# Retention part of a two-layer decoder: weight blocks asked for one ahead, head ends 24 products behind the sums, later modulations

## The chip, the cores and the metric

The kernel runs on 1 core of one Trainium2 chip. The metric is the device time of one execution in microseconds. Before the change the median of 3 runs is 2658.96 us (2655.59 to 2659.36).

## The reference

Two layers on a sequence of 256 rows of width 2048. Layer 0 mixes with retention (8 heads, key width 256, value width 512), layer 1 with a short gated convolution; each is followed by a SwiGLU part of width 5632. Every sub-layer is normalised, scaled and shifted by rows made from a conditioning vector `c`, and its output is multiplied by a gate made the same way.

```python
c_act = jax.nn.silu(c)
for i in range(DEPTH):
    mod = (c_act @ w_mod[i] + b_mod[i])[:, None, :]
    sh1, sc1, g1, sh2, sc2, g2 = jnp.split(mod, 6, axis=-1)
    h = (rms_norm(x, norm1_g[i]) * (1.0 + sc1) + sh1).astype(x.dtype)
    ...
    x = (x + g1 * y).astype(x.dtype)
    h = (rms_norm(x, norm2_g[i]) * (1.0 + sc2) + sh2).astype(x.dtype)
    x = (x + g2 * swiglu(h, ffn_w_in[i], ffn_w_out[i])).astype(x.dtype)

def retention_mixer(h, cos, sin, w_in, w_out):
    q, k, v, g = jnp.split(h @ w_in, [qk_w, 2 * qk_w, 2 * qk_w + v_w], axis=-1)
    q = rope(split_heads(q, RET_HEADS), cos, sin)
    k = rope(split_heads(k, RET_HEADS), cos, sin) * (RET_DK ** -0.5)
    v = split_heads(v, RET_HEADS)
    ...
    o = rms_norm(chunked_gated_linear_attention(q, k, v, log_a))
    return ((jax.nn.silu(g) * merge_heads(o)) @ w_out).astype(h.dtype)
```

## The kernel before

All activations lie with features on the 128 partitions and the 256 rows along the free axis, as 16 tiles. Two streams come from memory, both as 1 MB blocks of 128 x 2048 float32, all issued on SP's queue. `w_all` (456 blocks) holds every weight of a product in the order of use. `w_mod` (192 blocks) holds the matrix for the conditioning rows; each of these blocks is reduced to one column by a VectorE multiply-and-sum (L244, in `modulation`), followed by a small addition on GpSimd. 32 of them belong to the start; the other 160 are spread over the kernel by `paced`, which follows `plan_mod`: pairs of (units of product done, modulations due), interpolated between them. A unit is one product of a 128 x 128 weight tile; the retention part has 2048 of them. They are issued at lower priority (`MOD_PRIO`).

**The weight stream.** A product needs each weight in two parts. `prepare` takes half a block (1024 columns): ScalarE makes `hi` by a cast (L310), VectorE makes `lo = raw - hi` (L313). `take` keeps two halves (`AHEAD`) ready ahead of the one in use. `fetch` asks for a block: it takes the next of the 3 buffers of the tag `raw` (`RAW_BUFS`), whose turn goes round strictly, and issues the transfer on SP. The buffers of `w_mod` blocks have the same tag, so a block of either kind takes the buffer of the block three before it, and its transfer waits until that one's last reader is done. In the first spans (up to `early`) `prepare` asks for up to two blocks beyond the one in use; after that only when a block is needed.

**Order of work.** TensorE's order is written out by hand. VectorE's and ScalarE's orders are the scheduler's, except in the start and the first spans, where they are by hand too; every engine works through its own order in sequence. `product` runs two matmuls for each weight tile (L355 with hi, L358 with lo), `packed` three (L378, L379, L380), the values of a head three wide ones (L801, L802, L803).

**The retention part.** First some spans of columns of several heads (`RET_SPANS`, 480 units), while the rows are being normalised. Then the heads in the order 4, 0, 2, 1, 5, 3, 6, 7. `projections` does, for each head: the pair for q and its rotation (`rope`, L778 to L786 on VectorE), the pair for k, the values, the scores, two more pairs for the gate. What is left of a head, its *asides* from `mixed`, runs inside the next head's products: `outputs(0)` and `outputs(1)` (score times value, L847 and L850, and sums of squares), `roots` (sums over partitions on TensorE, L413; VectorE L422; the power on GpSimd, L424) and `ends` (L431 spreads the roots over the partitions; then for each of four tiles VectorE multiplies, L864, ScalarE casts, L394, and VectorE takes the rest, L395, into a `mid` tile named `rm`). `ticked`, called after every k step of a product with the number of products done, runs the next aside when so many have passed as its entry in `STEPS` says: 8, 8, 24, 12.

After four heads and after eight, `ret_out` multiplies by the output weights (`output`, `RET_OUT`): its first group makes 6 columns over 12 of the 16 k steps (72 products), while the last head's asides run; then a group for each of these columns adds the last 4 k steps, which read the four `rm` tiles of that last head; then the other columns follow over all 16.

Of the kernel before, what the change touches and what calls it, by code (L numbers as in the profile page):

```python
# [17 lines left out]
P = 128  # L18
D = 2048
S = 256  # L20
KT = D // P
# [24 lines left out]
MOD_LEAD = 64  # L46
MOST = 0.045
MOD_PRIO = -300
STEPS = (8, 8, 24, 12)
RAW_BUFS = 3  # L50
PART_BUFS = 4

# [80 lines left out]
def in_use_order():  # L133

    for g in RET_SPANS:
        yield "ret_w_in", 0, g
    for n, h in enumerate(HEAD_ORDER):
        qkg, v = RET_HEADS[h]
        for g in qkg[:2] + [v] + qkg[2:]:
            yield "ret_w_in", 0, g  # L140
        if n % (HEADS // 2) == HEADS // 2 - 1:
            for g in RET_OUT[n // (HEADS // 2)]:
                yield "ret_w_out", 0, g
    for layer in range(DEPTH):
        if layer == 1:
            for g in CONV_IN:
                yield "conv_w_in", 0, g
            for g in CONV_OUT:
                yield "conv_w_out", 0, g
        for part in range(2):  # L150
            for g in FFN_IN[part]:
                yield "ffn_w_in", layer, g
            for g in FFN_OUT[part]:
                yield "ffn_w_out", layer, g
# [31 lines left out]
def trunk(ctx: ExitStack, tc: tile.TileContext, x_in, c_in, pos_in, w_mod, cols_in, tab_in, w_all, out):  # L186
# [8 lines left out]
    def name(s):  # L195
        serial[0] += 1
        return f"{s}_{serial[0]}"
# [62 lines left out]
    n_mod = len(todo)  # L260
    todo.reverse()
    first = len(RET_SPANS[0].cols) * FIRST_KS
    early = sum(len(g.cols) * len(g.ks) for g in RET_SPANS)
    plan_mod = [(early, 0), (1024, 18), (1984, 49), (5184, 9 * KT), (5888, n_mod)]
    units, allowed = [0], [0.0]

    def paced(n):
# [19 lines left out]
    ready, taken_cols, raws, fetched, n_fetched = [], [0], [], [], [0]  # L287

    def fetch():
        raw = wpool.tile([P, CHUNK], F32, tag="raw", name=name("raw"), bufs=RAW_BUFS)  # L290
        nc.sync.dma_start(raw, w_all[n_fetched[0]])
        n_fetched[0] += 1
        fetched.append(raw)

    def prepare(between=None):
        n = prepared[0]
        if n == n_halves:
            return
        prepared[0] += 1
        i = n * HALF % CHUNK  # L300
        if i == 0:
            if not fetched:
                fetch()
            raws[:] = [fetched.pop(0)]
            while first <= units[0] < early and len(fetched) < RAW_BUFS - 1 and n_fetched[0] < w_all.shape[0]:
                fetch()
        raw = raws[0][:, i : i + HALF]
        hi = wpool.tile([P, HALF], F32R, tag="hi", name=name("hi"))
        lo = wpool.tile([P, HALF], F32R, tag="lo", name=name("lo"))
        nc.scalar.copy(hi, raw)  # L310
        if between:
            between()
        nc.vector.tensor_tensor(lo, raw, hi.bitcast(F32), op=ALU.subtract)  # L313
        ready.append((hi, lo))
# [3 lines left out]
    def take(group, k, col):  # L318

        assert order.pop() == (group, k, col)  # L320
        i = taken_cols[0] % HALF
        if i == 0:
            if ready and taken_cols[0]:
                ready.pop(0)
            while len(ready) < 1 + AHEAD * (units[0] >= first):
                n = len(ready)
                prepare()
                if len(ready) == n:
                    break
        taken_cols[0] += group.width  # L330
        return [t[:, i : i + group.width] for t in ready[0]]
# [211 lines left out]
    with ExitStack() as inner:  # L543
# [64 lines left out]
        with tc.tile_pool(name="start", bufs=1) as sp:  # L608
# [56 lines left out]
            with tc.manual_schedule(engines={mybir.EngineType.DVE, mybir.EngineType.Activation}):  # L665
# [59 lines left out]
                def before(k):  # L725
                    low = []
                    prepare(lambda: low.append(row(k)))
                    low[0]()

                pts = packed(RET_SPANS[0], h, before=before, between=both_reduced, banks=banks)  # L730
                prepare()
                prepare()
                for i, pt in enumerate(pts):
# [103 lines left out]
        def mixed(head, both, v, sg):  # L837
# [3 lines left out]
            def outputs(half):  # L841
                for i in range(2 * half, 2 * half + 2):
                    pt = bank()
                    w = slice(i * P, (i + 1) * P)
                    for jt, sp in enumerate(both):
                        at = slice(jt * P, S)
                        nc.tensor.matmul(  # L847
                            pt[:, :, at], v[:, jt, 0, w], sp, start=jt == 0, stop=False, skip_group_check=True
                        )
                        nc.tensor.matmul(  # L850
                            pt[:, 1, at], v[:, jt, 1, w], sp[:, 0, :], start=False, stop=jt == 1, skip_group_check=True
                        )
                    o = summed(pt, rp.tile([P, S], F32, tag="o", name=name("o"), bufs=4))
                    accs[0] = squares(accs[0], o, "hacc")
                    nc.vector.tensor_tensor(o, o, sg[i], op=ALU.mult)
                    os.append(o)
# [11 lines left out]

            return list(zip(STEPS, [lambda: outputs(0), lambda: outputs(1), roots, ends]))

# [153 lines left out]
```

## Time and profile before

| what | us |
|---|---|
| median of 3 runs | 2658.96 |
| profiled execution | 2658.37 |
| its span | 2656.6 |
| VectorE busy in the span | 2019.6 |
| ScalarE busy in the span | 1260.2 |
| L313, lo: 912 of them, mean | 1.223 |
| L310, hi: 912 of them, mean | 1.050 |
| L244, modulation: 160 of them, mean | 2.285 |
| block of `w_all`, issue to landing, median | 4.9 |
| block of `w_mod`, issue to landing, median | 5.2 |

The table is read from the page's first, fifth and sixth parts. Mean durations include the start-up of an instruction, which overlaps with its neighbour when they run back to back, so a row of three L313 in 3.49 us costs less than three times the mean. The granted clock of TensorE is 0.996 of full speed over the span. The transfers' queue took 69.4% of what 16 DMA engines could give.

In time, the first spans end at about 215 us, heads 4, 0, 2 and 1 run until 350 us, the first `ret_out` until 443 us, heads 5, 3, 6 and 7 until 709 us, and the second `ret_out` to about 800 us. A head's asides are at the start of its follower: L431 of head 4 stands at 250 us, of head 0 at 287, of head 2 at 335.7, of head 1 at 373.7 and of head 5 at 537.7.

### The profile page before, as it was taken

The page shows a single profiled execution, that of the slowest core. Times are in us where ns is not written, and L with a number is a line of the kernel's source. Part 1 is how long each engine was busy: PE and PEld are TensorE (multiplying, and loading weights), DVE is VectorE, ACT ScalarE, POOL GpSimd, SP SyncE. Part 2 cuts the span into 40 slices and gives each one's busy share as a digit, 9 for nine tenths or more (in the row PEclk, how much of TensorE's full clock was granted, in tenths as well). Part 3 has the DMA queues.
Part 4 walks back from the last instruction along what each step waited for, and adds up shares of the span by engine and source line. Part 5 has one row for each costly group of instructions (what it writes and reads, how often), then busy time and mean ns, then how long its engine had stood idle before and what let it go on. Part 6 is the DMA issues. An engine that isn't in the chain of part 4 may idle for free.

```text
span 2656.6 us, 40105 instructions
## 1 busy us (share of the span) xinstructions
PE 2619.1 (99%) x16044; PEld 2337.2 (88%) x16044; DVE 2019.6 (76%) x2646; ACT 1260.2 (47%) x1819; POOL 152.5 (6%) x230
## 2 busy tenths in 40 slices
PE   7999999999999999999999999999999999999998
PEld 6998889889889888888888898888988888888887
DVE  7888988787699877777777889878887665555554
ACT  5545543444456444344444454444554443444443
POOL 0000000120000011100000001100000000000000
PEclk9999999999999999999999999999999999999999
DMA  9975668777676877877777758777777765555553
GB/s 396 396 274 221 221 234 317 260 271 280 242 272 252 322 282 262 300 268 279 283 278 274 274 218 322 288 276 262 264 267 260 263 222 190 187 185 185 188 190 127
DMA packets 96958, 687.70 MB, mean 259 GB/s; under 512 B 10753, under 2 KB 12545, under 8 KB 13825
## 3 DMA queue, kind: packets, MB, share of 16 engines
q1 hardware_dynamic: 96770, 685.13, 69.4%
q8 instruction: 125, 2.05, 0.3%
q14 instruction: 63, 0.52, 0.1%
HBM read 682.99 MB, written 2.10 MB: 258 GB/s over the span
## 4 chain that ended last, share of the span: by engine, by line
PE 75%; issue 19%; DVE 3%; DMA 2%; ACT 0%; POOL 0%; DVEq 0%; SPq 0%; ACTq 0%; POOLq 0%
PE bank L355 35%; PE bank L358 17%; PE bank L380 4%; PE bank L378 4%; PE bank L379 4%; PE bank L802 2%; PE bank L803 2%; PE bank L801 2%; PE bank L494 1%; PE bank L493 1%; PE bank L495 1%; DMA raw<-w_all 1%; DVE lo L313 1%; DMA raw<-w_mod 0%; DVE raw L244 0%
## 5 line engine op out<-in xcount | busy, mean ns | idle before, releaser
L313 DVE TENSOR_TENSOR lo<-raw,hi 128x1024 fp32r<-128x1024 f32 x912 | 1112.1, 1223 | 548.1 <-ACT hi L310 544.1
L310 ACT CAST hi<-raw 128x1024 fp32r<-128x1024 f32 x912 | 953.9, 1050 | 1099.7 <-PE bank L355 630.8
L355 PE MATMUL bank<-h,hi 128*128 128x512 f32 x3296 | 1155.2, 395 | 0.0
L358 PE MATMUL bank<-h,lo 128*128 128x256 f32 x3296 | 924.4, 280 | 0.0
L355 PEld LDWEIGHTS bank<-h,hi 128*128 128x128 f32 x3296 | 622.6, 189 | 145.3
L358 PEld LDWEIGHTS bank<-h,lo 128*128 128x128 f32 x3296 | 622.0, 189 | 0.0
L355 PE MATMUL bank<-mid,hi 128*128 128x512 f32 x1604 | 556.3, 393 | 0.0
L358 PE MATMUL bank<-mid,lo 128*128 128x256 f32 x1604 | 444.9, 277 | 0.0
L244 DVE SCALAR_TENSOR_TENSOR raw<-raw,cb 128x2048 f32<-128x2048 f32 x160 | 365.6, 2285 | 10.8 <-DMA raw<-w_mod 10.3
L355 PEld LDWEIGHTS bank<-mid,hi 128*128 128x128 f32 x1604 | 300.7, 187 | 69.4
L358 PEld LDWEIGHTS bank<-mid,lo 128*128 128x128 f32 x1604 | 301.3, 188 | 0.1
L380 PE MATMUL bank<-h,lo 128*128 128x256 f32 x1024 | 291.1, 284 | 7.5 <-DVE lo L313 7.5
L378 PE MATMUL bank<-h,hi 128*128 128x256 f32 x1024 | 291.0, 284 | 3.6 <-ACT h L644 3.6
L379 PE MATMUL bank<-h,hi 128*128 128x256 f32 x1024 | 290.2, 283 | 0.0
L380 PEld LDWEIGHTS bank<-h,lo 128*128 128x128 f32 x1024 | 194.9, 190 | 8.3 <-DVE lo L313 8.3
L378 PEld LDWEIGHTS bank<-h,hi 128*128 128x128 f32 x1024 | 196.5, 192 | 3.9 <-ACT h L644 3.9
L379 PEld LDWEIGHTS bank<-h,hi 128*128 128x128 f32 x1024 | 195.1, 191 | 0.2 <-DVE h L645 0.2
L355 PE MATMUL bank<-rm,hi 128*128 128x512 f32 x496 | 174.8, 397 | 0.1
L358 PE MATMUL bank<-rm,lo 128*128 128x256 f32 x496 | 138.5, 279 | 0.0
L355 PEld LDWEIGHTS bank<-rm,hi 128*128 128x128 f32 x496 | 93.1, 188 | 22.2 <-DVE rm L395 0.4
L802 PE MATMUL bank<-lo,h 128*128 128x512 f32 x256 | 101.8, 398 | 4.1 <-DVE lo L313 4.1
L801 PE MATMUL bank<-hi,h 128*128 128x512 f32 x256 | 102.1, 399 | 0.0
(155 smaller groups left out, 2187.2 us busy)
## 6 DMA issues: line engine op xcount, KB each, us to landing
raw<-w_all SPq DMA_DIRECT2D x456, 1024.0 KB, 4.9
raw<-w_mod SPq DMA_DIRECT2D x192, 1024.0 KB, 5.2
x<-x_in SPq DMA_DIRECT2D x4, 512.0 KB, 5.7
out<-out SPq DMA_DIRECT2D x5, 256.0 KB, 2.9
decay<-tab_in SPq DMA_DIRECT2D x8, 128.0 KB, 3.6
out<-out SPq DMA_DIRECT2D x3, 128.0 KB, 2.3
out<-out SPq DMA_DIRECT2D x1, 384.0 KB, 2.7
cols<-cols_in SPq DMA_DIRECT2D x1, 160.0 KB, 8.7
```

The costliest lines, as they stand in the source:

```text
L244: nc.vector.scalar_tensor_tensor(raw, raw, 1.0, cb, op0=ALU.mult, op1=ALU.mult, accum_out=total)
L310: nc.scalar.copy(hi, raw)
L313: nc.vector.tensor_tensor(lo, raw, hi.bitcast(F32), op=ALU.subtract)
L355: nc.tensor.matmul(pt, hi, h, start=fresh and k == g.ks[0], stop=False, skip_group_check=True)
L358: nc.tensor.matmul(pt[:, 1, :], lo, h[:, 0, :], start=False, stop=last and k == g.ks[-1], skip_group_check=True)
L378: nc.tensor.matmul(pt, hi, h[:, 0, :], start=first, stop=False, skip_group_check=True)
L379: nc.tensor.matmul(pt, hi, h[:, 1, :], start=False, stop=False, skip_group_check=True)
L380: nc.tensor.matmul(pt, lo, h[:, 0, :], start=False, stop=last, skip_group_check=True)
L493: nc.tensor.matmul(pt, hi, rows[0], start=k == 0, stop=False)
L801: nc.tensor.matmul(o, ht[:, 0, :], hi, start=k == 0, stop=False)
L802: nc.tensor.matmul(o, ht[:, 0, :], lo, start=False, stop=False)
L803: nc.tensor.matmul(o, ht[:, 1, :], hi, start=False, stop=k == KT - 1)
```

## The change

It has three parts. The last entry of `STEPS` goes from 12 to 24, so `ends` follows `roots` by 24 products. In `plan_mod` the early modulations have a later due time: 0 at 480 units as before, then 8 at 912 units and 18 at 1168, where it was 18 at 1024; from 1984 units on it is as before. In `prepare`, the number of blocks asked for beyond the one in use is 2 up to `early` as before, and then 1 up to the end of the retention part (2048 units), where it was none. In the order of the changed kernel, the number of modulations that stand before the ends of each head is 1, 3, 5, 6, 23, 28, 35, 40, where it was 2, 5, 8, 10, 27, 32, 38, 42. The number of instructions on every engine is the same.

```diff
-STEPS = (8, 8, 24, 12)
+STEPS = (8, 8, 24, 24)
...
-    plan_mod = [(early, 0), (1024, 18), (1984, 49), (5184, 9 * KT), (5888, n_mod)]
+    ret_units = sum(len(g.cols) * g.width // P * len(g.ks) for key, _, g in in_use_order() if key[:3] == "ret")
+    plan_mod = [(early, 0), (ret_units // 2 - 7 * KT, 8), (ret_units // 2 + 9 * KT, 18), (1984, 49), (5184, 9 * KT), (5888, n_mod)]
...
-            while first <= units[0] < early and len(fetched) < RAW_BUFS - 1 and n_fetched[0] < w_all.shape[0]:
+            most = RAW_BUFS - 1 if units[0] < early else 1
+            while first <= units[0] < ret_units and len(fetched) < most:
                 fetch()
```

## The prediction

> **What bounds the kernel now.** The page's first part says which engine sets the time. The span is 2656.6 us; the profiled execution took 2658.37 us, 0.6 below the median 2658.96. All sums below are made against 2658.4, and 0.6 is added at the end. Two runs count as different from 0.2% on (5.3 us), about what a measurement of this kernel can tell from no change.
>
> ```profile
> PE 2619.1 (99%) x16044; PEld 2337.2 (88%) x16044; DVE 2019.6 (76%) x2646; ACT 1260.2 (47%) x1819; POOL 152.5 (6%) x230
> ```
>
> PE is idle for 2656.6 - 2619.1 = 37.5 us, and the edit removes no matrix product. So it can only win idle PE time, and only in the retention part, since the order on every engine is unchanged up to about 215 us and from about 810 us. The view of waits says what ended PE's idle times (total, count, longest):
>
> ```profile
> PE bank L380 <- DVE lo L313: 7.5, 4, 2.7
> PE bank L802 <- DVE lo L313: 4.1, 2, 2.2
> PE bank L431 <- POOL rs L424: 3.6, 3, 1.5
> PE bank L378 <- ACT h L644: 3.6, 1, 3.6
> PE bank L847 <- DVE sp L395: 0.8, 1, 0.8
> ```
>
> The four at L380 and the one at L378 lie before 58 us, out of reach. In reach are: L802 twice (326.54, 1.86 us; 526.75, 2.24 us), L431 twice (285.49, 1.47; 584.70, 1.12; the third is at the kernel's end), L847 (230.94, 0.77), and 0.09 at 738.60 before L355. With some 0.17 us of refilling each, they cost about 8.4 us. The windows view (engines, then granted clock, DMA share, GB/s) adds one thing:
>
> ```profile
> 325.00:330.00 5.00, 3.14 (x14) 2.27 (x13) 5.00 (x9) 1.96 (x3) 0.00 (x0) 1.00 0.00 0
> 525.00:530.00 5.00, 2.76 (x11) 1.93 (x10) 4.98 (x11) 2.19 (x4) 0.00 (x0) 0.87 0.05 11
> 500.00:550.00 50.00, 47.76 (x304) 43.03 (x303) 37.97 (x58) 21.40 (x33) 8.52 (x9) 0.97 0.65 234
> ```
>
> In both 5 us rows DVE is full while PE waits for it. After the 2.24 us gap the clock falls (0.97 over 50 us: half speed for some 3.4 us, so 1.7 us lost); after 1.86 us it stays at 1.00. All that can be won is thus 8.4 + 1.7 = 10.1 us, 0.38%.
>
> Why DVE was late there is in the chain of waits (start, length, what):
>
> ```profile
> 511.54 6.90 DMA raw<-w_mod
> 518.56 2.30 DVE raw L244 x2
> ...
> 525.76 0.69 DVE q L786
> 526.45 0.34 DVE hacc L405
> 526.85 0.19 issue
> 527.04 0.42 DVE hacc L405
> 527.46 0.33 DVE o L855
> 527.79 1.15 DVE lo L313
> 528.98 0.79 PE bank L802
> ```
>
> A modulation L244 waits for its block; DVE works in order, so the rope, the outputs' sums and then the lo that PE needs come behind it.
>
> **The change, gains.** (Line numbers are of the kernel before; the changed one has 1 to 2 more.) The ends go from 12 to 24 products after the roots; a value tick of 4 products is 6 matmuls of 0.23 us, so 12 products are 4.15 us. L431 waited 1.47 and 1.12 us for POOL's root; 4.15 more covers both: 1.65 + 1.29 = 2.9 us. With weight blocks asked for one ahead, the lo that PE missed at 526.75 stands 21 rows earlier on DVE, before rope and sums: 2.4 us and the clock's 1.7, 4.1 in all. The lo of 326.54 moves up 27 rows: 2.0 us. At 738.60 0.3 goes. L847 stays, as nothing ahead of it changes. Sum of gains 9.3 us. Fewer modulations early (one to four fewer before each of the first heads' ends, the 160 and their 2.29 us unchanged in total) lighten DVE before 374 us by 4 x 2.29 = 9 us, hidden as DVE is not the bound there.
>
> **Losses at ret_out.** Its first group makes 6 columns x 12 k-steps = 72 products while the last head's asides run after 8, 8, 24 and the new 24 ticks. Ticks come in sixes, so 12 + 12 + 24 + 24 = 72: L431 now stands directly in front of the first product that reads what ends makes. Before, 12 products (4.15 us) lay between, and even so the second part stalled a little. The steps are these (timeline of DVE):
>
> ```profile
> 586.57 1.08 DVE L864 TENSOR_TENSOR o<-o,bank 128x256 f32<-128x256 f32 x3 [1.36 <-PE bank L431]
> 587.57 0.76 DVE L395 TENSOR_TENSOR rm<-o,rm 128x256 fp32r<-128x256 f32 x2
> 588.24 0.41 DVE L864 TENSOR_TENSOR o<-o,bank 128x256 f32<-128x256 f32 x1
> ```
>
> Let T be the end of the 72nd product. L864 starts at T+0.75 (here 585.82 to 586.57). ACT has a hi ahead of the first rm, as its order stands (1.05 us, from T+0.31 on), so rm follows at T+1.3, its DVE half at T+1.7, and the product starts at T+2.2 where T+0.5 was possible: 1.7 us. DVE then does three L395, L864, a lo (1.14) and only then the fourth L395, done at T+4.5, while PE is ready for it three products of 0.35 us after T+2.2: 1.4 us more. So 3.1 us per part, two parts: 6.2 us; bounds 1.7 x 2 = 3.4 (the fourth hidden) and 9.5 (each with a clock drop of 1.7).
>
> **Losses at the blocks.** The three raw buffers rotate strictly: a block's DMA is issued only when the tile three before it has been read. With a block one ahead, w_all and w_mod tiles alternate differently, and some w_all blocks inherit the buffer of a w_mod tile, that is, wait for L244, which DVE reaches late. SP hands out requests in order, so a request that waits for its buffer also holds those behind it, the modulations' among them; POOL's small adds behind L244 only come later and nothing here waits for them. I walked the engines' orders with durations of these rows (hi 1.05, lo 1.14, L244 2.29, 1 MB in 4.9 us).
> During head 3's values, a block takes the buffer of an L244 ending near 535.5: landing 540.5, hi and lo done near 542.9, wanted at 541.2: 1.7 us (0.5 to 3), and 0.3 as two L244 stand before head 5's ends.
> During head 6's products, a modulation's DMA goes out only after a lo at 585 and lands near 591.5; behind its L244 stand head 3's ends, rope and a lo wanted at 597.9, done at 600. The next block takes that buffer, lands near 605, and its lo is done near 607 where 600.7 was wanted. The least is the first lo's 2.1 and its refilling, 2.5 us; the most 7; I take 5.7, nearer the upper end, as the second block's transfer can't start before the first lo is done.
> During head 1's values, an L244 whose block lands late (near 314) holds DVE for some 3.4 us; the last hacc sum is done at 329.9, L413 stands at 327.6: 2.3 us (0 to 2.5). This gives back the 2.0 won there.
> Every new stall near 2 us can drop the clock, as at 526.75. Before 58 us gaps of 2.67 and 2.04 did, 1.86 and less did not here. Of four to six new stalls of 1.7 to 6 us, I take two drops of 1.7: 3.4 us; bounds 0 and 6.8.
>
> [...]
>
> **Sum.** -9.3 + 6.2 + 2.0 + 5.7 + 2.3 + 3.4 = +10.3 us: 2658.4 + 10.3 = 2668.7, and with the median's 0.6, 2669.3. I say 2669. The small ends of all losses (3.4 + 0.5 + 2.5 + 0 + 0 = 6.4) leave -2.9, the large ones (6.2 + 3.3 + 7 + 2.5 + 6.8 = 25.8) +16.5 on the other side.
>
> **Rivals.**
> First, the early request works as it reads: the five gaps go and no block is late, since being asked for one ahead gives each the sixteen products of the block in use, 16 x 0.35 = 5.6 us, against 4.9 us of transfer. For it: the DMA queue is busy 69.4% of the time, and DVE had room up to 374 us. Against it: the buffers' turn, not the request, sets when a transfer starts. Of the losses only ret_out's first wait stays, 3.4 us: 2659.0 - 9.3 + 3.4 = 2653 us, faster. It decides if the block stalls are under 1 us together. Chance 0.16.
> Second, it balances: all gains, ret_out's 6.2 and some 3 us of block stalls: 2659.0 - 9.3 + 6.2 + 3 = 2659 us. For it: the block stalls are the least certain terms, while ret_out's follow from the order alone. Against it: three of them have a cause that stands in the orders. Chance 0.16.
> Third, the request does little, as the buffer that it asks for is still held where it matters: the gaps at 326 and 526 stay, those of L431 and at 738 go, ret_out's 6.2 comes: 2659.0 - 2.9 - 0.3 + 6.2 = 2662 us. Against it: both lo stand 21 and 27 rows earlier on DVE. Chance 0.06.
> The forecast has the rest, 0.62. It is slower by over 0.2%; the second and third are within it, 0.22; the first is faster, 0.16. The range, 2652 to 2680, reaches from the first rival's time past the losses' large ends (2659.0 + 16.5 = 2675.5) by one more stall of the head 6 kind; the likeliest case's own is 2664.5 to 2678.
>
> **What would show it.** Right: a PE gap of about 1.7 us before L355 at the end of both 72-product groups, then one of about 1.4 three products later, ended by DVE rm; no gap at L431 in heads' products; a gap at L380 or L802 ended by lo, with a w_mod transfer or L244 in the chain before it, in the products after head 3's and head 5's values; more than one half-clock stretch past 58 us. Wrong: PE busy with no gap over 1 us between 490 and 620, or ret_out's wait under 1 us (then the rm came earlier than ACT's order lets me think), or a new wait at a line that I did not walk.

## The result and the profile after

The changed kernel takes 2668.13 us (median of 7 runs, 2665.12 to 2677.16) against 2658.96 us: ratio 1.004, with an interval of 1.003 to 1.005. It is slower by 9.2 us. Its profiled execution took 2671.37 us with a span of 2669.6 us, 13.0 longer than the span before; it is one of its longer executions, 3.2 us over the median. Where places are given below, lines of the changed kernel have numbers 2 higher than before (L433 is L431 of before, L357 is L355, L804 is L802, L495 is L493, L397 is L395).

The first part of the page, then the view of waits of TensorE (what it waited for, total us, times, longest):

```profile
PE 2626.1 (98%) x16044; PEld 2344.1 (88%) x16044; DVE 2021.0 (76%) x2646; ACT 1260.2 (47%) x1819; POOL 146.1 (5%) x230
```

```profile
PE bank L382 <- DVE lo L315: 7.9, 6, 3.2
PE bank L495 <- ACT h L481: 6.2, 1, 6.2
PE bank L357 <- DVE rm L397: 5.3, 4, 1.5
...
PE bank L433 <- POOL rs L426: 1.0, 1, 1.0
...
PE bank L849 <- DVE sp L397: 0.8, 1, 0.8
```

The waits for lo in the values (L802 before, L804 now) are gone. So are two of the three for the root (the 1.0 left is at the kernel's end) and the 0.09 us at ret_out's old place. Those gaps were 1.47 + 1.86 + 2.24 + 1.12 + 0.09 = 6.8 us. In their place are four waits for rm, 5.3 us; one of 6.2 us at a line that waited for nothing before, the first products of the FFN (the SwiGLU part that follows); and two of the six at L382 and one for hi that lie just after the first ret_out (0.76, 0.22 and 0.90 us near 446 to 456). New gaps together: 13.4 us. With 0.6 us less in the start, idle time grew by 13.4 - 6.8 - 0.6 = 6.0 us.

PE's busy time rose by 2626.1 - 2619.1 = 7.0 us for the same matmuls. Most of that is clock, as the windows view shows (engines' busy time, then granted clock, DMA share, GB/s):

```profile
325.00:330.00 5.00, 5.00 (x25) 4.14 (x24) 4.91 (x9) 2.14 (x3) 2.29 (x1) 1.00 0.08 13
370.00:380.00 10.00, 7.33 (x37) 6.05 (x36) 6.18 (x13) 3.54 (x6) 0.00 (x0) 0.89 0.42 155
440.00:455.00 15.00, 13.34 (x88) 12.49 (x87) 10.53 (x13) 3.36 (x5) 0.38 (x2) 0.89 0.80 300
500.00:550.00 50.00, 50.00 (x336) 46.01 (x335) 42.37 (x60) 23.49 (x35) 10.35 (x11) 1.00 0.72 265
735.00:745.00 10.00, 7.35 (x31) 5.94 (x30) 7.98 (x16) 3.50 (x6) 0.19 (x1) 0.73 0.37 143
800.00:820.00 20.00, 13.82 (x94) 13.42 (x93) 12.73 (x20) 6.57 (x10) 0.50 (x2) 0.83 0.75 284
```

The rows 325 and 500 are full now (3.14 of 5 and 47.76 of 50 before). The four others have a gap and, behind it, a stretch at half clock: the trace's clock records have half of full speed granted for 3.4 us from 377.7 on, 3.4 from 449.4, 6.8 from 739.5 and 6.8 from 811.2, while the ones of 3.4 us at 57.7 and 528.7 of the profile before are not there. That is 13.7 us more at half speed. PE was itself waiting in 3.5 us of the new stretches, so on balance they cost some 5 us of work; the rest of the 7.0 is the refilling after the new gaps and small differences that were not traced one by one. (Refilling is an estimate from rows of the kernel before: between 324.8 and 326.5 us the matmuls of L801 to L803 last 0.39 us each and start 0.23 us apart, so PE counts as busy some 0.16 us longer for each gap.) Idle and busy time together, 6.0 + 7.0, are the 13.0 us by which the spans differ.

The wait at ret_out, as DVE's timeline shows it (start, length, line):

```profile
373.84 1.08 DVE L866 TENSOR_TENSOR o<-o,bank 128x256 f32<-128x256 f32 x3 [1.02 <-PE bank L433]
374.84 1.09 DVE L397 TENSOR_TENSOR rm<-o,rm 128x256 fp32r<-128x256 f32 x3
375.84 0.42 DVE L866 TENSOR_TENSOR o<-o,bank 128x256 f32<-128x256 f32 x1
376.18 1.22 DVE L315 TENSOR_TENSOR lo<-raw,hi 128x1024 fp32r<-128x1024 f32 x1
377.31 0.42 DVE L397 TENSOR_TENSOR rm<-o,rm 128x256 fp32r<-128x256 f32 x1
```

PE stood still from 373.80 to 375.31, when the first rm was done, ran three products, and stood still again from 376.63 to 377.78 for the fourth, which has a lo ahead of it.

The wait at the FFN's start, from the chain of waits:

```profile
809.64 1.22 DVE lo L315
810.86 2.21 DVE raw L244 x2
813.64 0.58 PE bank L495
```

The last of the 48 modulations that the FFN's first rows need is this L244. DVE's timelines have it, in the kernel before and in the changed one:

```profile
786.30 2.28 DVE L244 SCALAR_TENSOR_TENSOR raw<-raw,cb 128x2048 f32<-128x2048 f32 x1
```

```profile
810.78 2.28 DVE L244 SCALAR_TENSOR_TENSOR raw<-raw,cb 128x2048 f32<-128x2048 f32 x1
```

Before the change it began 16 us before PE came to these products at 802; now it begins when PE, which came at 807.47, is already waiting. GpSimd's addition (813.15) and ScalarE's cast (L481, 813.37) follow, and PE begins at 813.6.

### The profile page after: what moved, and what is told of

Read it like the earlier page. It is cut to its first block, busy times and chain, and to the rows that moved or that the text cites. A ratio compares the mean times of both kernels' runs of the same rounds, so it can differ in the third digit from the quotient of the medians.

```text
span 2669.6 us, 40114 instructions
## 1 busy us (share of the span) xinstructions
PE 2626.1 (98%) x16044; PEld 2344.1 (88%) x16044; DVE 2021.0 (76%) x2646; ACT 1260.2 (47%) x1819; POOL 146.1 (5%) x230
## 4 chain that ended last, share of the span: by engine, by line
PE 76%; issue 19%; DMA 2%; DVE 1%; ACT 1%; SPq 0%; POOL 0%; DVEq 0%; ACTq 0%; POOLq 0%
PE bank L357 34%; PE bank L360 17%; PE bank L382 4%; PE bank L380 4%; PE bank L381 4%; PE bank L803 2%; PE bank L804 2%; PE bank L805 2%; PE bank L495 1%; DMA raw<-w_all 1%; PE bank L496 1%; PE bank L497 1%; DMA raw<-w_mod 1%; DVE lo L315 1%; PE bank L849 0%
## 5 line engine op out<-in xcount | busy, mean ns | idle before, releaser
L357 PE MATMUL bank<-h,hi 128*128 128x512 f32 x3296 | 1155.2, 395 | 0.0
L357 PEld LDWEIGHTS bank<-h,hi 128*128 128x128 f32 x3296 | 623.1, 189 | 144.4
L357 PE MATMUL bank<-mid,hi 128*128 128x512 f32 x1604 | 556.3, 394 | 0.0
L244 DVE SCALAR_TENSOR_TENSOR raw<-raw,cb 128x2048 f32<-128x2048 f32 x160 | 365.7, 2286 | 17.9 <-DMA raw<-w_mod 17.8
L357 PEld LDWEIGHTS bank<-mid,hi 128*128 128x128 f32 x1604 | 301.2, 188 | 69.7
L382 PE MATMUL bank<-h,lo 128*128 128x256 f32 x1024 | 292.3, 285 | 7.9 <-DVE lo L315 7.9
L382 PEld LDWEIGHTS bank<-h,lo 128*128 128x128 f32 x1024 | 195.7, 191 | 9.1 <-DVE lo L315 9.1
L357 PE MATMUL bank<-rm,hi 128*128 128x512 f32 x496 | 179.9, 406 | 5.3 <-DVE rm L397 5.3
L357 PEld LDWEIGHTS bank<-rm,hi 128*128 128x128 f32 x496 | 95.3, 192 | 29.2 <-DVE rm L397 6.3
L803 PE MATMUL bank<-hi,h 128*128 128x512 f32 x256 | 101.9, 398 | 0.0
L804 PE MATMUL bank<-lo,h 128*128 128x512 f32 x256 | 101.0, 394 | 0.0
```

The lines of the kernel that those rows point to most:

```text
L244: nc.vector.scalar_tensor_tensor(raw, raw, 1.0, cb, op0=ALU.mult, op1=ALU.mult, accum_out=total)
L357: nc.tensor.matmul(pt, hi, h, start=fresh and k == g.ks[0], stop=False, skip_group_check=True)
L382: nc.tensor.matmul(pt, lo, h[:, 0, :], start=False, stop=last, skip_group_check=True)
L803: nc.tensor.matmul(o, ht[:, 0, :], hi, start=k == 0, stop=False)
L804: nc.tensor.matmul(o, ht[:, 0, :], lo, start=False, stop=False)
```

## The experiments

All ratios are to runs of the kernel before on the same chip (medians 2658.04 us for the first four, 2657.68 us for the last four). So an experiment is set beside the changed kernel by how far each is from its own runs of before; for the changed kernel that is 9.2 us. Line numbers are those of before in e1, 1 higher in e3 and e8, and those of the changed kernel in the others.

**e1: the fourth step alone.**

```diff
-STEPS = (8, 8, 24, 12)
+STEPS = (8, 8, 24, 24)
```

> The kernel before with the fourth step 24 in place of 12 alone. Theory (the step sets ret_out's waits): TensorE waits twice in both ret_out parts, about 1.5 and 1.15 us each before L355, ended by DVE rm, as in the changed kernel (5.3 us of gaps, 6.0 with the refilling), and half-clock stretches follow them (1.7 us lost for each 3.4 us stretch); the two waits at L431 inside heads' products (1.47 and 1.12 us) are gone, the waits for lo at L802 (1.86 and 2.24 us) stay. Together +3 to +8 us against before. Rival (the waits at ret_out come from the weight blocks or the modulations): no wait over 0.3 us before L355 at ret_out, and -2 to -3 us.

Measured: 2663.42 us, ratio 1.0020 (1.0012 to 1.0029). The waits for rm came, 1.51 and 1.15 us at the first ret_out and 2.61 and 0.45 at the second:

```profile
PE bank L355 <- DVE rm L395: 5.7, 4, 2.6
PE bank L378 <- ACT h L644: 3.7, 1, 3.7
PE bank L802 <- DVE lo L313: 2.8, 2, 2.4
```

No wait at L431 is left inside heads' products. So the step alone makes ret_out's waits, and costs 5.4 us, inside the 3 to 8 of the theory. The waits for lo at L802 stay (2.40 and 0.42 us), and a new one of 0.69 us at L413 came.

**e2: the early request alone.**

```diff
-            while first <= units[0] < early and len(fetched) < RAW_BUFS - 1 and n_fetched[0] < w_all.shape[0]:
+            most = RAW_BUFS - 1 if units[0] < early else 1
+            while first <= units[0] < ret_units and len(fetched) < most:
```

> The kernel before with the weight block asked for one ahead alone. Theory A (the early request wins the gaps for lo, and the later plan causes the 6.2 us wait of the FFN's first products): the waits at L802 near 327 and 527 us are gone, the wait for ACT h at the FFN's start is under 1 us, the time is 3 to 7 us below before. Theory B (the block asked for early holds buffers back from the modulations and so makes the 6.2 us wait): that wait is 4 to 7 us here too, and the time is 2 to 7 us above before. Small waits for lo or hi near 446 us belong to the early request in both.

Measured: 2661.11 us, ratio 1.0009 (1.0000 to 1.0018). The time, 3.1 us above before, lies in theory B's range, but B's cause is absent: there is no wait at the FFN's start, as theory A says. Nor are there small waits near 446, which both theories put down to the request. The request alone wins too little: the wait near 527 is gone, the one near 325 is longer (3.05 us), and there is one for the root of 3.37 us at 533, with half clock behind it (granted clock 0.90 from 530 to 540 us):

```profile
PE bank L433 <- POOL rs L426: 5.2, 3, 3.4
...
PE bank L804 <- DVE lo L315: 3.0, 1, 3.0
```

**e3: the later plan alone.**

```diff
-    plan_mod = [(early, 0), (1024, 18), (1984, 49), (5184, 9 * KT), (5888, n_mod)]
+    plan_mod = [(early, 0), (ret_units // 2 - 7 * KT, 8), (ret_units // 2 + 9 * KT, 18), (1984, 49), (5184, 9 * KT), (5888, n_mod)]
```

> The kernel before with the later plan of modulations alone. Theory A: 8 modulations in place of 6 are left behind the last head's ends, so the FFN's first products wait 4 to 7 us for ACT h, with a half-clock stretch: +5 to +10 us against before. Theory B (the early request makes that wait): no wait over 1 us there, and the time is within 3 us of before. The waits at L802 for lo stay in both, as the request is as before.

Measured: 2660.08 us, ratio 1.0008 (0.9999 to 1.0017). The place of the wait is that of theory A. Its size and the time are below A's ranges; the time, 2.0 us above before, is in theory B's:

```profile
PE bank L494 <- ACT h L480: 3.5, 1, 3.5
...
PE bank L803 <- DVE lo L314: 1.3, 1, 1.3
```

The FFN's start waits 3.48 us, and 0.55 more; the wait for lo near 327, which was to stay, is gone, and the one near 527 is down to 1.32 us. It is the lighter plan and not the early request that removed the wait near 327.

**e4: the changed kernel with the fourth step back at 12.**

```diff
-STEPS = (8, 8, 24, 24)
+STEPS = (8, 8, 24, 12)
```

> The changed kernel with the fourth step back at 12. Theory: the four waits for rm at ret_out (5.3 us) and the half-clock stretches behind them (10 us at half speed in the profile of the changed kernel, 5 us lost) go, while the wait at the FFN's start and the small ones near 446 us stay: 6 to 11 us below the changed kernel, so 2657 to 2662 us. L431 may wait again, 1 to 1.5 us once or twice. Rival (the waits move to the next late thing): less than 3 us below the changed kernel.

Measured: 2666.51 us, ratio 1.0027 (1.0018 to 1.0036), against 1.004 (1.003 to 1.005). By the medians it is 8.5 us above before, 0.7 less than the changed kernel; the ratios give some 3 us less, with intervals that overlap. Both are near the rival's less than 3 and far from the theory's 6 to 11. The waits for rm went, but two others took their room: the root's at L433 (1.44, 2.09 and 1.34 us) and a longer one at the FFN's start:

```profile
PE bank L495 <- ACT h L481: 8.1, 1, 8.1
PE bank L433 <- POOL rs L426: 5.9, 4, 2.1
```

PE came to the FFN at 803.8, 3.7 us earlier, while the last modulation's L244 began at 809.0, only 1.8 earlier.

**e5: the changed kernel with the plan caught up.** Six modulations are left behind the last head's ends, as before, in place of eight.

```diff
-..., (ret_units // 2 + 9 * KT, 18), (1984, 49), ...
+..., (ret_units // 2 + 9 * KT, 22), (1984, 49), ...
```

> The changed kernel with 22 in place of 18 modulations due at 1168 units, so that 42 stand before the last head's ends, as before the change, and 6 are left behind them, not 8. Theory (the wait at the FFN's start is the last shift modulation coming late, by the two that the plan left behind): two L244 of this stretch are 6 us apart, so the 48th comes some 12 us earlier, near 799 us, and the 6.2 us wait for ACT h and its half-clock stretches are gone; the waits at ret_out stay. 6 to 10 us below the changed kernel: 2658 to 2662. Rival (the buffers that the early request holds make it, whatever the plan): a wait of 3 us or more stays there.

Measured: 2661.16 us, ratio 1.0013 (1.0004 to 1.0022). That is 3.5 us above before, 5.7 less than the changed kernel's 9.2 and just under the 6 that was the least expected. The 48th L244 begins at 792.3 and the FFN's start does not wait. The waits for rm stay, and three small ones for lo come back at L804, 1.3 us in all, with one of 0.39 us for hi.

**e6: the changed kernel with the fourth step 12 for the heads that end in ret_out.**

```diff
-            return list(zip(STEPS, [lambda: outputs(0), lambda: outputs(1), roots, ends]))
+            steps = STEPS[:3] + (12 if head in HEAD_ORDER[3::4] else STEPS[3],)
+            return list(zip(steps, [lambda: outputs(0), lambda: outputs(1), roots, ends]))
```

> The changed kernel with the fourth step 12 for the two heads that end inside ret_out (1 and 7) and 24 for the other six. Theory: no wait for rm over 0.3 us at ret_out, no wait at L433 in heads' products. That is 5.3 us of gaps and about 5 us of clock, but the wait at the FFN's start grows by some 2 us, as it did (6.2 to 8.1) with the fourth step at 12 everywhere: 4 to 9 us below the changed kernel, 2659 to 2664. Rival (what ret_out gives back is lost in full at the FFN): within 2 us of the changed kernel.

Measured: 2660.79 us, ratio 1.0017 (1.0008 to 1.0025). That is 3.1 us above before, 6.1 less than the changed kernel. Between the start and 840 us only two gaps are left, the 0.85 us at L849 and the one of the FFN, 7.1 us long:

```profile
PE bank L495 <- ACT h L481: 7.1, 1, 7.1
...
PE bank L849 <- DVE sp L397: 0.9, 1, 0.9
```

```profile
370.00:380.00 10.00, 10.00 (x59) 8.69 (x58) 8.84 (x18) 4.73 (x8) 0.00 (x0) 1.00 0.53 191
535.00:545.00 10.00, 10.00 (x48) 8.24 (x48) 9.00 (x13) 7.40 (x12) 0.00 (x0) 1.00 0.85 305
590.00:600.00 10.00, 10.00 (x45) 8.07 (x44) 8.05 (x7) 4.10 (x4) 0.48 (x2) 1.00 0.98 378
790.00:810.00 20.00, 12.92 (x92) 12.72 (x91) 11.34 (x18) 5.51 (x9) 1.07 (x3) 0.83 0.68 261
```

PE is without a gap in the first three rows: at ret_out, and at the two places where the prediction had late blocks. In the last one it loses 7.1 us to the wait and, with a granted clock of 0.83 over these 20 us, at most 3.4 us more to the clock (0.17 x 20). Without ret_out's waits the small waits near 446 are gone too, though nothing of the early request was changed.

**e7: both edits on the changed kernel** (those of e5 and e6).

> Both edits on the changed kernel: 22 due at 1168 units, and the fourth step 12 for heads 1 and 7 alone. Theory: neither the waits at ret_out nor the one at the FFN's start nor those for lo at L804 nor those at L433; what is left in the retention part is L849 (0.85 us) and perhaps 1 to 2 us near 446. 3 to 9 us below before: 2650 to 2656. Rival (late blocks under the early request take the place of the waits removed): 2657 to 2663.

Measured: 2654.47 us, ratio 0.9987 (0.9978 to 0.9996), inside the theory's range at its upper part, 3.2 us faster than before. What is left between 440 and 800 us are five gaps of 0.2 to 0.8 us, 2.4 us in all; the granted clock is 0.997 over the span, against 0.994 in the changed kernel. Two of the five are waits for lo at L804 (0.52 and 0.77 us), of which the theory had none.

**e8: the kernel before with the plan of e5 and the steps of e6, without the early request.** The edits are those two on the kernel before; `prepare` is as before.

> The kernel before with the later plan (22 due at 1168 units) and the fourth step 24, but 12 for heads 1 and 7, and with no block asked for ahead. Theory (the early request is not what won the waits for lo; the lighter plan won the one near 327 us): no wait there, none at L431, one of 1 to 2.3 us for lo near 527 us, none over 1 us at the FFN's start: 2 to 5 us below before. Rival (the early request is needed): waits for lo of 3 us or more in all, and not below before.

Measured: 2653.85 us, ratio 0.9986 (0.9977 to 0.9995), as fast as e7. It waits 1.60 us for lo near 526, which e7 doesn't, and 1.4 us in five small waits. So of the three parts of the change the early request wins nothing that can be measured once the other two are set right. e7 and e8 can't be told apart, and both are faster than the two kernels of this study, if only by some 0.13% of the time before.

## Why the prediction was right, and where it was not

**The gains (9.3 us) held.** All the gaps named are gone, 6.8 us and their refilling, and so is the half-clock stretch at 528.7. The gaps at L431 go with the step (e1). One of the gaps was put down to the wrong part: the lo near 327 was to be won by the early request, but e2 has a wait of 3.05 us there and e3 none. The lighter plan did it. The prediction had costed the lighter plan at nothing, "hidden as DVE is not the bound there", though its own row of 325 to 330 us had DVE full while PE waited.

**ret_out (3.1 us per part) held.** It said 1.7 us and then 1.4; the gaps are 1.51 and 1.15, in both parts, with refilling some 3.0. e1 has them with the step alone, and e6 loses them by setting the step back for two heads. The steps of the walk (L433, multiply, cast behind a hi, subtract; a lo ahead of the fourth) stand in the timeline in that order.

**The late blocks (2.0 + 5.7 + 2.3 us) did not come.** In the changed kernel no product between 480 and 700 us waits, nor does L415 near 328. The half block that was to be 1.7 us late in head 3's values was done 0.61 us before its first use; the one of head 6's that was to be some 6 us late was done 2.84 us before. e6 rules out that ret_out's waits merely hid the lateness: there PE is 8.5 us earlier at these places, and the two margins are again 0.61 and 2.84 us. The step that failed is "The three raw buffers rotate strictly: a block's DMA is issued only when the tile three before it has been read." The section on the kernel before says the same of the buffers' turn, and it holds in neither kernel. The timelines of DVE and of SP's queue in the changed kernel show otherwise:

```profile
535.95 1.23 DVE L315 TENSOR_TENSOR lo<-raw,hi 128x1024 fp32r<-128x1024 f32 x1
537.09 2.29 DVE L244 SCALAR_TENSOR_TENSOR raw<-raw,cb 128x2048 f32<-128x2048 f32 x1
539.30 0.09 DVE L244 DVE_READ_ACCUMULATOR raw<-raw,cb 128x1 f32 x1
```

```profile
537.25 4.71 SPq L292 DMA_DIRECT2D raw<-w_all  x3
```

The tile three before the weight block of head 3's values is the modulation whose L244 ends at 539.30, and the walk made the block wait for it. Its transfer went out at 537.25, just behind the lo before it: it took the buffer of the block that this lo had read. The next two went out at 539.41 and 541.63, behind the two L244. At head 6 the block that was to wait for a lo near 600 was issued behind an L244 that ended at 590.65:

```profile
588.36 2.29 DVE L244 SCALAR_TENSOR_TENSOR raw<-raw,cb 128x2048 f32<-128x2048 f32 x1
590.57 0.08 DVE L244 DVE_READ_ACCUMULATOR raw<-raw,cb 128x1 f32 x1
```

```profile
590.68 0.33 SPq L292 DMA_DIRECT2D raw<-w_all  x1
```

The block three before it was read until 596.39. The kernel before did the same: a weight block went out at 585.23, behind an L244 that ended at 585.20, while the block three before it was read until 589.79. In these rows each block took the buffer that came free next in DVE's order, and no modulation lying idle held up the block behind it. An estimate from these rows shows what the wrong rule was worth: had the two blocks waited as the walk had it, 2.2 and 5.7 us longer, the margins of 0.61 and 2.84 us would have become 1.5 and 2.9 us of lateness, near the 1.7 that the walk gave head 3 and half of what it gave head 6. Beside that the walk's times were off by 2 us at head 6: the transfer that was to go out behind a lo at 585 went out at 583.1. The places were tight all the same: with the modulations of e5 and e7, two or three more by these heads, waits of 0.2 to 0.8 us appear at them.

**The wait that was not on the list.** "POOL's small adds behind L244 only come later and nothing here waits for them" is the step that failed here: PE's wait of 6.2 us ends behind such an addition. And "the order on every engine is unchanged up to about 215 us and from about 810 us" is true of the order and says nothing of the times. The plan leaves eight modulations and not six between the last head's ends and the FFN's first rows, and their L244 come 6 to 10 us apart in this stretch. The prediction priced what a lighter plan frees and not the point where the deferred work is wanted. The runs settle whose it is: with neither part the 48th L244 begins at 786.3, with the early request alone at 792.0, with the plan alone at 796.8, with both at 809.0 (e4) and 810.8. Only the runs with eight left wait, and with six left (e5, e7, e8) none does. The request adds to it: 8.1 us in e4 against 3.5 and 0.6 in e3, which differ in the request alone, and the 48th comes 3 us earlier in e8 than in e7, which differ in it alone too. (e1, the step alone, has six left and no wait either.) SP's queue shows one way in which it adds. Where six are left, 126 weight blocks go out before the 48th modulation's transfer without the request (before, e1, e8) and 127 with it (e2, e5, e7); where eight are left, 129 without (e3) and 130 with it (e4, e6, the changed kernel). So with the request one more weight block has the turn before that modulation. How many of the microseconds come from this was not tried by itself.

By the prediction's own list two signs of being wrong came: PE has no gap over 1 us between 490 and 620 us, and there is a new wait at a line that was not walked.

**The sum.** +10.3 us was forecast and 2669 named; the medians differ by 9.2. The direction was right, and the gains and ret_out's losses are its sound part. That the sum came out within about 1 us is luck, as the other terms were others: the 10.0 us of late blocks did not come, and 6.2 us at the FFN and 1.9 near 446, with refilling and clock, did. The clock was taken at two drops, 3.4 us, with 6.8 as the upper bound; in the profiled execution the new stretches came to 20.5 us at half speed (two are of double length), some 8.5 us of work lost beside PE's own waits in them. The removed stretches at 57.7 and 528.7 give back some 3.2; the one at 57.7 is not the change's doing, as the last section shows. That profile is 3.8 us further from before than the medians are.

The three parts alone cost 5.4, 3.1 and 2.0 us, 10.5 in all; together 9.2. They nearly add up, but not place by place: the FFN's wait is 0 with the early request, 4.0 with the plan, 8.1 with both and 6.2 with all three.

## What to carry to other kernels

When work is deferred, look up who reads its last piece and count the pieces that are left behind the last point where there is room: the cost shows where that reader stands, which may be hundreds of microseconds from the edit. A number of steps that covers a latency inside a long run of products covers nothing where it just reaches the first reader; e6 and e7 keep it for the heads where products follow and take it back where the run ends. And a walk of queues is only as good as its rule for buffers: look in the trace which release each transfer follows before a wait is built on it.

## What the runs showed of the hardware

The clock records of the two kernels' traces begin at 23.5 us (before) and 26.1 us (changed). In each trace the records of half clock start whole multiples of 3.413 us apart: 44.019 and 528.711 of the kernel before are 142.0 such steps apart, 43.211 and 811.210 of the changed kernel 225.0. PE's idle time in the one step ahead of each of them was:

| trace | half clock from, us | for, us | PE idle in the 3.413 us ahead, us |
|---|---|---|---|
| before | 44.0 | 3.4 | 2.03 |
| before | 57.7 | 3.4 | 1.89 |
| before | 528.7 | 3.4 | 1.97 |
| before | 2645.0 | 13.6 | 1.04 |
| changed | 43.2 | 3.4 | 3.24 |
| changed | 377.7 | 3.4 | 2.09 |
| changed | 449.4 | 3.4 | 1.66 |
| changed | 739.5 | 6.8 | 1.65 |
| changed | 811.2 | 6.8 | 3.41 |
| changed | 2661.2 | 10.4 | 1.02 |

The 1.66 are two waits near 447 together, 0.90 and 0.76 us; the 1.65 are 1.51 and the first 0.14 of the next near 738. Of the steps at full clock with no half clock behind them, the one with the most idle time past 45 us has 1.11 us in the kernel before (near 585) and 1.49 in the changed one (near 58), and one near 25 us of the kernel before has 1.68. So 1.68 us left the clock alone once and 1.02 brought it down at a kernel's end: no one amount parts the two in these traces, and what else decides was not shown.

The length of a wait does not part them either. The kernel before waited 2.04 us up to 57.8 and half clock followed (granted clock 0.76 from 55 to 62 us), with 1.89 of the wait in one step; the changed kernel waited 2.02 us up to 58.4, cut into 0.53 and 1.49 by a border of its steps, and kept its clock (1.00 from 55 to 62). So these two executions, with nearly the same wait, differ there by one stretch of 3.4 us at half speed, some 1.7 us of work. In e2 a wait of 3.05 us left the clock at 1.00:

```profile
322.00:330.00 8.00, 4.96 (x22) 3.74 (x21) 7.97 (x16) 3.07 (x5) 0.00 (x0) 1.00 0.05 5
```

In e5 the same pair of waits at ret_out had both outcomes, a clock of 1.00 at the first and of 0.66 at the second:

```profile
370.00:380.00 10.00, 7.34 (x42) 6.04 (x41) 6.73 (x13) 3.54 (x6) 0.00 (x0) 1.00 0.41 119
735.00:745.00 10.00, 7.41 (x25) 6.14 (x26) 7.82 (x15) 4.46 (x10) 0.19 (x1) 0.66 0.50 190
```
